# Branch projections as seven block products per pair of output tiles, with weight sums formed in DRAM, on one Trainium2 core

## The chip, the cores and the metric

The kernel runs on one core of a Trainium2 chip. The metric is the device time of one execution in microseconds (us). Before the change the median of 3 runs was 1196.73 us (1196.19 to 1196.98).

## What is computed

One layer of a decoder with 1024 positions and 1024 channels, in float32. The reference, cut to what the change touches:

```python
proj = h @ w_in[l]                      # h = rmsnorm(x)
q, k, v, su, sv, g_a, g_b = jnp.split(proj, splits, axis=-1)
y_att = sliding_window_attention(q, k, v, ...)         # 1024 x 512
y_sgu = chunked_spatial_gating(su, sv, ...)            # 1024 x 512
merged = (jax.nn.sigmoid(g_a) * (y_att @ w_oa[l])      # branch a
          + jax.nn.sigmoid(g_b) * (y_sgu @ w_ob[l]))   # branch b
x = x + merged @ w_out[l]
x = x + conv_gated_mlp(rmsnorm(x, ffn_norm[l]), ...)
```

The change rewrites the two products `y_att @ w_oa` and `y_sgu @ w_ob`, each 1024 x 512 by 512 x 1024.

## The kernel before, in words

Everything is kept transposed: channels on the 128 partitions, positions along the free dimension. A float32 product is made of three TensorE matmuls in the fp32r format: operands are split into a high part (`copy_hi`, ACT, L87) and a low part (operand minus high part, one subtraction on DVE or POOL), and `mm3` (L91 to L93) adds high·high, high·low and low·high in PSUM. One matmul is 128x128 by 128x512. PSUM is used as four rotating tiles of 128x1024 float32 (`PS`).

The program is written under a manual schedule: on each engine the instructions stand in the order in which the code issues them, and each engine runs its own list in that order. The stages, one after the other on TensorE:

1. Attention, the spatial gate and the input projections other than the gates (to about 247 us).
2. Gate projections, "gate pairs" 1 to 7 (`gate_pair`, called from `gates`). Each pair makes one tile of gate a (`zv`) and one of gate b (`zg`) by seven block products instead of eight (class `Blocks`, L1039 issues its matmuls; 12 matmuls in a product, 84 in a pair). Between products there are copies of PSUM halves to SBUF on ACT (`x1`, `x7`, `u2`; L1099, L1105, L1049), sums on DVE (L620, L1048, L1058), a scale on DVE (L1055) and a tanh on ACT (L1068, `gate_out`); the tanh goes to DRAM until its branch tile is merged. During pair 7, which has no successor to prepare, the right sides of the branch projections are split: `ys_split` for branch b (`bh` on ACT, `bl` on DVE, L1144) and `ya_split` for branch a (`ah` on ACT, `al` on POOL, L1144), four times 128x1024 each.
3. Branch projections: 16 jobs (`branch`), one tile of 128 output channels each, in the order b, b, a, a. A job is a plain contraction over 512 channels (`dense`: 4 steps of 128 channels, two halves of 512 positions, 3 matmuls: 24). DVE then multiplies by one plus the tanh (L1190, L1192), adds the two branches (L1193), and the merged tile is split again for the next stage (`m_split`: `mh` on ACT, `ml` on DVE, L1204).
4. Output projection: 8 jobs (`out_tile`) of 48 matmuls (L91 to L93, tile `px`), each followed by the residual sum, the norm's square and the splits for the MLP (`right_split`).
5. The MLP's up projection in block products (`first_pair`, then `fast_pair`, whose copies to `x1` and `x7` are L1501 and L1518), and the down projection.

`run_jobs` drives stages 3 and 4: job i's matmuls are issued, then job i + 4's weights are loaded (SP queue, tile `wj`) and job i + 2's are split (`wjh` on ACT, L87; `wjl` on POOL, L108), then the rest of job i.

Two things of the machine's use matter for reading the change. PSUM accumulation: in `Blocks` the product "A12·B21" is added onto the half `g0` that holds "A11·B11", after ACT has copied "A11·B11" out to `x1`; in the same way "A22·T4" is added onto `v0` after the copy to `x7`. TensorE therefore waits at its third product for ACT's copy `x1`, and at its fifth for `x7`. And in `fast_pair` ACT's copy to `x7` stands behind `nx.split_s3()`, the split of the next pair's weights.

Of the kernel before, what the change touches and what calls it, by code (L numbers as in the profile page):

```python
# [10 lines left out]
F = mybir.dt.float32  # L11
# [30 lines left out]
def body(ctx, tc, nc, a):  # L42
# [658 lines left out]
    def job_load(i):  # L701
        if i < len(jobs):
            src, nk, _ = jobs[i]
            job_w[i] = wload(src, "wj", nk) if nk else first_left()
            if not nk:
                next(job_w[i])

    def job_split(i):
        if i < len(jobs):
            nk = jobs[i][1]  # L710
            if nk:
                job_w[i] = wsplit(job_w[i], "wj", nk)
            else:
                for _ in job_w[i]:
                    pass
# [74 lines left out]
    def v_phase():  # L790
# [8 lines left out]
        for s in range(7):  # L799
# [5 lines left out]
            v_gelu(s)  # L805
            if s < 4:
                nc.scalar.activation(uT[:, s, :], uT[:, s, :], AF.Gelu_apprx_tanh)
# [15 lines left out]
    def v_end():  # L823
# [3 lines left out]
        v_half(7, 1)  # L827
        sgu_mm(1, 0)
# [70 lines left out]
    pools = {"dr": dr}  # L899

# [30 lines left out]
    class Left:  # L931
# [15 lines left out]
        def load_ahead(self):  # L947

            if "lq" not in pools:
                pools["lq"] = U("lq", F, (128, 2, 2048))  # L950
# [71 lines left out]
    class Blocks:  # L1022


        def __init__(self, w, y, z=None):
            self.w, self.y = w, y
            self.rest(z or (PS("pz"), PS("pz")))
# [7 lines left out]
        def prod(self, o, l, r, more=False):  # L1035
            (wh, wl), y = self.w[l], self.y[r]
            for k in range(4):
                for j, (p, q) in enumerate(((wh, 0), (wh, 1), (wl, 0))):
                    nc.tensor.matmul(o, p[:, k, :], y[:, q, k, :], start=not more and k == 0 and j == 0,  # L1039
                                     stop=k == 3 and j == 2, skip_group_check=True)  # L1040
# [39 lines left out]
    def gates_close():  # L1080
# [4 lines left out]
        pools["mg"] = pools["mg_cm"].__enter__()  # L1085

    def gate_pair(c, prev):
# [15 lines left out]
        gate_out(("b", c - 1), prev.zg)  # L1103
        q.prod(q.v0, "S3", "T3")
        nc.scalar.copy(x7, q.v0)  # L1105
        q.prod(q.g0, "A12", "B21", more=True)
# [4 lines left out]
        else:  # L1111
            ys_split()
            job_split(0)
            job_load(2)
        q.prod(q.g1, "S1", "T1")
        sub(nc.vector, x7, x7, q.g1)
        if nx:
            nx.sums_r()
        q.prod(q.v0, "A22", "T4", more=True)
        if nx:  # L1120
            nx.split_q()
        else:
            job_split(1)
            ya_split()
# [12 lines left out]
    yb = {}  # L1137

    def y_split(n, t, src, eng):
        if n not in yb:  # L1140
            yb[n] = Y(n + "h"), Y(n + "l")
        h, l = yb[n]
        copy_hi(h[:, t, :], src)
        eng.tensor_tensor(l[:, t, :], src, h[:, t, :].bitcast(F), op=ALU.subtract)  # L1144

    def ys_split():
        for t in range(4):
            y_split("b", t, uT[:, t, :], nc.vector)
# [5 lines left out]

    def ya_split():
        for t in range(4):
            y_split("a", t, yb["raw"][:, t, :], nc.gpsimd)

    def gates():
# [6 lines left out]
        for key in B_ORDER[:2]:  # L1166
            th_load(key)


    B_ORDER = [(br, c + e) for c in range(0, 8, 2) for br in "ba" for e in (0, 1)]  # L1170
    ms = {}

    def th_load(key):
        th[key] = pools["ls"].tile([128, 1024], F, tag="th", name=nm("th"), bufs=3)
        nc.sync.dma_start(th[key], d_th[key])

    def branch(n):
        br, c = B_ORDER[n]

        def main(w):  # L1180
            if n + 2 < 16:
                th_load(B_ORDER[n + 2])
            yh, yl = yb[br]
            p = PS("po")
            dense(p, *w, lambda k: yh[:, k, :], lambda k: yl[:, k, :], 4)
            yield
            t = th.pop((br, c))
            if br == "b":
                ms[c] = pools["mg"].tile([128, 1024], F, tag="m", name=nm("m"), bufs=3)
                nc.vector.scalar_tensor_tensor(ms[c], t, 1.0, p, op0=ALU.add, op1=ALU.mult)  # L1190
            else:
                nc.vector.scalar_tensor_tensor(p, t, 1.0, p, op0=ALU.add, op1=ALU.mult)  # L1192
                nc.vector.tensor_tensor(ms[c], ms[c], p, op=ALU.add)  # L1193
                m_split(c)
        jobs.append((a["wob" if br == "b" else "woa"][c], 4, main))
# [3 lines left out]
    def m_split(c):  # L1199
        if mhi[c // 4] is None:  # L1200
            mhi[c // 4], mlo[c // 4] = Y("mh"), (Y if c < 4 else U)("ml")
        h, l = mhi[c // 4][:, c % 4, :], mlo[c // 4][:, c % 4, :]
        copy_hi(h, ms[c])
        nc.vector.tensor_tensor(l, ms.pop(c), h.bitcast(F), op=ALU.subtract)  # L1204

    for n in range(16):
        branch(n)
# [4 lines left out]
    def open_out():  # L1212
# [4 lines left out]
        pools["ex"] = ctx.enter_context(tc.tile_pool(name="ex", bufs=1, reuse_waits="tile"))  # L1217
# [4 lines left out]
        comb["T3"] = pools["ex"].tile([128, 2, 4, 512], R, tag="T3", name="T3")  # L1222
# [6 lines left out]
        out_load(D_ORDER[0])  # L1229
# [15 lines left out]
    def out_tile(i):  # L1245
        d = D_ORDER[i]

        def main(w):
            if i == 0:
                open_out()  # L1250
            if i < 7:
                out_load(D_ORDER[i + 1])
            sq2, ac = pools["sq2"], acs.pop(d)
# [579 lines left out]
```

## Time and profile before

| what | value |
|---|---|
| median of the runs | 1196.73 us (1196.19 to 1196.98) |
| the profiled execution's own time | 1196.83 us |
| its span, first to last instruction | 1195.1 us |
| branch projections on TensorE (384 matmuls) | 380.6 to 467.7 us |
| gate pair 7 on TensorE (84 matmuls) | 361.5 to 380.6 us |
| output projection on TensorE (384 matmuls) | 467.7 to 554.9 us |
| busy share of the span | DVE 70%, ACT 45%, POOL 50% |

The page of the profile gives the busy time of each engine, the chain of work that ended last and the costliest groups of instructions; the trace behind it can be asked for single waits, groups of instructions and stretches of time. Times there count from the first instruction. The profiled execution's time is 1.7 us above its span.

### The profile page before, as it was taken

What the parts mean: (1) busy time and instruction counts of PE and PEld (TensorE: products, weight loads), DVE (VectorE), ACT (ScalarE), POOL (GpSimd) and SP (SyncE); (2) the same over time, 40 slices, a digit from 0 to 9 for tenths busy, and PEclk for the clock granted to TensorE, in tenths of its full rate; (3) what the DMA queues carried; (4) which work ended last, traced back from release to release, by engine and by line L of the source; (5) the groups of instructions that cost most, each with busy time, mean ns of one, the idle gap of its engine ahead of it and who ended that gap; (6) DMA issues with size and microseconds to landing.
All of it is one profiled execution on the core that took longest, in us unless ns stands there. A gap on an engine that the chain in (4) does not pass through costs nothing.

```text
span 1195.1 us, 15765 instructions
## 1 busy us (share of the span) xinstructions
PE 1181.0 (99%) x5890; PEld 1000.1 (84%) x5890; DVE 834.6 (70%) x984; ACT 540.9 (45%) x832; POOL 596.7 (50%) x408
## 2 busy tenths in 40 slices
PE   8999999999999999999999999999999999999998
PEld 8989989988888888888788888888888888888887
DVE  7798975752325453678787788878887798775674
ACT  8555567644435122235444435444444445434331
POOL 2367684587686222344777676767767551000000
PEclk9999999999999999999999999999999999999999
DMA  7110143024343634353555555545545358975472
GB/s 273 34 54 19 54 142 124 13 94 141 108 174 106 219 134 159 124 175 110 129 159 138 135 166 134 167 119 146 155 137 146 92 203 282 367 247 194 151 227 72
DMA packets 72797, 173.97 MB, mean 146 GB/s; under 512 B 8208, under 2 KB 8464, under 8 KB 72720
## 3 DMA queue, kind: packets, MB, share of 16 engines
q1 hardware_dynamic: 66384, 161.42, 39.0%
q0 software_dynamic: 6336, 11.54, 6.5%
q8 instruction: 46, 0.75, 0.3%
q14 instruction: 31, 0.25, 0.1%
HBM read 133.87 MB, written 39.06 MB: 145 GB/s over the span
## 4 chain that ended last, share of the span: by engine, by line
PE 85%; DVE 5%; POOL 2%; ACT 1%; issue 1%; DMA 0%; POOLq 0%; ACTq 0%; DVEq 0%
PE pz L1039 43%; PE pd L1659 10%; PE pdy L1659 8%; PE px L92 2%; PE po L93 2%; PE po L92 2%; PE px L93 2%; PE px L91 2%; PE po L91 2%; PE pvs L92 1%; PE pvs L91 1%; PE pvs L93 1%; PE pu L93 1%; PE pu L91 1%; PE pu L92 1%
## 5 line engine op out<-in xcount | busy, mean ns | idle before, releaser
L1039 PE MATMUL pz<-T,qh 128*128 128x512 f32 x472 | 145.7, 390 | 1.7 <-ACT x L1518 1.7
L1039 PE MATMUL pz<-B,ph 128*128 128x512 f32 x352 | 109.7, 393 | 0.2
L1039 PEld LDWEIGHTS pz<-T,qh 128*128 128x128 f32 x472 | 88.4, 188 | 20.7 <-ACT x L1518 2.1
L999 POOL TENSOR_TENSOR pl<-lp,ph 128x1024 fp32r<-128x1024 f32 x30 | 73.1, 2437 | 54.4 <-ACT ph L87 54.4
L1039 PE MATMUL pz<-T,ql 128*128 128x512 f32 x236 | 91.8, 389 | 0.0
L108 POOL TENSOR_TENSOR wjl<-wj,wjh 128x512 fp32r<-128x512 f32 (+1 forms) x24 | 39.9, 1663 | 99.1 <-ACT wjh L87 94.9
L999 POOL TENSOR_TENSOR ql<-lq,qh 128x1024 fp32r<-128x1024 f32 x30 | 76.6, 2552 | 9.1 <-ACT qh L87 9.1
L1039 PEld LDWEIGHTS pz<-B,ph 128*128 128x128 f32 x352 | 65.0, 188 | 16.6 <-ACT x L1501 3.8
L1055 DVE TENSOR_TENSOR pz<-pz,rstd_b 128x1024 f32<-128x1024 f32 x60 | 73.9, 1232 | 4.6 <-ACT rstd_b L141 2.5
L1039 PE MATMUL pz<-T,s3h 128*128 128x512 f32 x232 | 71.4, 389 | 0.0
L1039 PE MATMUL pz<-B,pl 128*128 128x512 f32 x176 | 68.6, 390 | 0.0
L1659 PE MATMUL pd<-bh,ah 128*128 128x512 f32 x176 | 68.5, 389 | 0.0
L1659 PE MATMUL pd<-bh,al 128*128 128x512 f32 x176 | 68.5, 389 | 0.0
L1659 PE MATMUL pd<-bl,ah 128*128 128x512 f32 x176 | 68.5, 389 | 0.0
L1039 PE MATMUL pz<-T,AX 128*128 128x512 f32 x264 | 63.4, 389 | 0.0
L1039 PE MATMUL pz<-B,AX 128*128 128x512 f32 x264 | 63.4, 389 | 0.0
L1039 PEld LDWEIGHTS pz<-T,AX 128*128 128x128 f32 x264 | 49.5, 188 | 10.3
L1039 PEld LDWEIGHTS pz<-B,AX 128*128 128x128 f32 x264 | 49.6, 188 | 10.3
L999 POOL TENSOR_TENSOR s3l<-lq,s3h 128x512 fp32r<-128x512 f32 x20 | 25.9, 1296 | 63.0 <-ACT s3h L87 63.0
L1359 DVE SCALAR_TENSOR_TENSOR tg<-pz,cp,tg 128x1023 f32<-128x1023 f32 (+1 forms) x44 | 56.2, 1277 | 0.8
L1359 DVE SCALAR_TENSOR_TENSOR tv<-pz,cp,tv 128x1023 f32<-128x1023 f32 (+1 forms) x44 | 56.2, 1277 | 0.8
L87 ACT ACTIVATE AX<-lr 128x1024 fp32r<-128x1024 f32 x22 | 23.4, 1063 | 71.0 <-POOL lr L620 71.0
(344 smaller groups left out, 3547.5 us busy)
## 6 DMA issues: line engine op xcount, KB each, us to landing
lp<-wup SPq DMA_DIRECT2D x22, 512.0 KB, 3.8
lq<-wup SPq DMA_DIRECT2D x22, 512.0 KB, 4.0
ra<-wdown SPq DMA_DIRECT2D x44, 256.0 KB, 4.5
b<-T SPq DMA_DIRECT2D x44, 256.0 KB, 3.8
lq<-wup POOLq DMA_DIRECT2D x42, 256.0 KB, 5.2
B<-tv SPq DMA_DIRECT2D x33, 256.0 KB, 2.0
T<-tt SPq DMA_DIRECT2D x33, 256.0 KB, 2.2
b<-B SPq DMA_DIRECT2D x33, 256.0 KB, 3.2
```

What stands on the lines that cost most here:

```text
L87: return nc.scalar.activation(dst, src, AF.Copy, scale=scale)
L91: nc.tensor.matmul(out, wh, mh, start=first, stop=False, **kw)
L92: nc.tensor.matmul(out, wh, ml, start=False, stop=False, **kw)
L93: nc.tensor.matmul(out, wl, mh, start=False, stop=last, **kw)
L108: nc.gpsimd.tensor_tensor(l[:, :nk, :], r[:, :nk, :], h[:, :nk, :].bitcast(F), op=ALU.subtract)
L999: nc.gpsimd.tensor_tensor(l, r, h.bitcast(F), op=ALU.subtract)
L1039: nc.tensor.matmul(o, p[:, k, :], y[:, q, k, :], start=not more and k == 0 and j == 0, stop=k == 3 and j == 2, skip_group_check=True)
L1055: nc.vector.tensor_tensor(z, z, rstd_b, op=ALU.mult)
L1359: nc.vector.scalar_tensor_tensor(t[:, j:], p[:, 0:1024 - j], cw[:, ci, 2 - j:3 - j], t[:, j:], op0=ALU.mult, op1=ALU.add)
L1659: nc.tensor.matmul(o[d], p[:, k - k0, m], q[:, k - k0, :], start=new and k == 0 and j == 0, stop=k == HK - 1 and j == 2, skip_group_check= ...
```

## The change

1. **Branch projections.** The 16 jobs become 8 units, in the order b, a, b, a and so on. A unit makes two neighbouring output tiles of one branch by seven block products with 2 steps of 128 channels: 7 x 6 = 42 matmuls, where two jobs of before had 48. It is two jobs: the first with the products A11·B11, S3·T3, A12·B21 and S1·T1, the second with A22·T4, S2·T2 and S4·B22. Between them stand the copies `x1`, `x7` and `u2` on ACT (L1280, L1282, L1299 of the changed kernel) and the sums on DVE; PSUM tiles are called `pz` here too.
2. **Weight sums.** S1 to S4 come from DRAM. `wb_copy` copies the 512 KB blocks of the weights to a DRAM tile (8 times, on ACT's queue, in stage 1); `wb_add` adds the other blocks onto it by accumulating transfers (6, on POOL's queue, one in each of the gate pairs 1 to 6).
3. **Right sides.** The seven right sides of each branch (B11, B21, B22, T1 to T4) are sums of quarters (`y_sum`, DVE, 128x1024 each) and are split by `y_split` (`copy_hi` on ACT, the low part on DVE or POOL; L1213). Branch b's sums stand in gate pairs 3 to 6; branch a's sums and ten of the fourteen splits in gate pair 7; the last four splits (a: T3, T1, T2, T4) behind pair 7 in `gates`, ahead of the first unit.
4. **Merge and output tiles.** The low parts of the merged tiles go to POOL in halves, one job later (`m_add`, `m_lo`), those of the last unit stay on DVE. Output tiles 0 and 1 are first contracted over steps 0 to 5 of 8, then over 6 and 7 (`rest`), and the split of job 18 moves.
5. **MLP's start.** The buffers `T3` and `lq` trade places. `lefts[2].load_ahead()` and `adds()` stand earlier in `first_pair`, and in the first call of `fast_pair` (`rms` set) the copy to `x7` stands ahead of `nx.split_s3()`.

Gate pair 7 and the first unit on **ACT**. `bh`, `ah` and `y...` are high parts of right sides, `uT`, `ya` and `yt` their sources, `wjh` the high parts of weights, `x`, `u` the copies of PSUM halves, `th` the tanh of a gate tile. Before, from the copy `x7` of pair 7 to the first weights of the branch stage:

```order
L1105 COPY x_498_3913<-pz_3911 128x512
L87 ACTIVATE bh_3965<-uT_683 128x1024 x4
L87 ACTIVATE wjh_3975<-wj_3929 128x512
L87 ACTIVATE wjh_4006<-wj_3931 128x512
L87 ACTIVATE ah_4010<-ya_3741 128x1024 x4
L1049 COPY u_499_3914<-pz_3911 128x512
L1068 ACTIVATE th_4039<-pz_3911 128x1024
L1068 ACTIVATE th_4057<-pz_3910 128x1024
L87 ACTIVATE wjh_4099<-wj_3979 128x512
```

And now, from the last weights split in pair 7 to the first unit's two copies (L1280 is its `x1`, L1282 its `x7`):

```order
L87 ACTIVATE wjh_4046<-wj_3959 128x256
L1068 COPY u_502_3939<-pz_3936 128x512
L87 ACTIVATE y_515_4072<-uT_683 128x1024
L87 ACTIVATE y_515_4072<-yt_3694 128x1024
L1087 ACTIVATE th_4081<-pz_3936 128x1024
L87 ACTIVATE y_519_4097<-uT_683 128x1024
L87 ACTIVATE y_519_4097<-ya_3764 128x1024
L1087 ACTIVATE th_4105<-pz_3935 128x1024
L87 ACTIVATE y_524_4123<-ya_3764 128x1024 x2
L87 ACTIVATE y_525_4128<-ya_3764 128x1024 x2
L1280 COPY x_528_4135<-pz_4133 128x512
L1282 COPY x_529_4136<-pz_4134 128x512
```

Between pair 7's last tanh (`th_4105`) and the first unit's copies there now stand four splits of 128x1024; the tanh tiles themselves now have splits between them.

The same place on **DVE**. `bl` and the second name of `y` rows are low parts; `ya<-ya` rows are the sums of branch a; `pz` rows with L1048/L1067, L620 and L1058/L1077 are pair 7's sums in PSUM, those with `rstd_b` its scales. Before, all of pair 7's tail up to the first merge of a branch tile (L1190):

```order
L1144 TENSOR_TENSOR bl_3966<-uT_683,bh_3965 128x1024 x4
L620 TENSOR_TENSOR x_498_3913<-x_498_3913,pz_3910 128x512
L1048 TENSOR_TENSOR pz_3911<-x_497_3912,pz_3911 128x512
L620 TENSOR_TENSOR pz_3911<-pz_3911,u_499_3914 128x512
L620 TENSOR_TENSOR pz_3911<-x_498_3913,pz_3911 128x512
L1055 TENSOR_TENSOR pz_3911<-pz_3911,rstd_b 128x1024
L1058 TENSOR_TENSOR pz_3910<-u_499_3914,pz_3910 128x512
L1055 TENSOR_TENSOR pz_3910<-pz_3910,rstd_b 128x1024
L1190 SCALAR_TENSOR_TENSOR m_4103<-th_4066,po_4072 128x1024
```

And now, in two pieces that follow each other, from the first split to the scale of `zv`:

```order
L1213 TENSOR_TENSOR y_507_3983<-uT_683,y_507_3983 128x1024
L1213 TENSOR_TENSOR y_507_3983<-yt_3560,y_507_3983 128x1024
L620 TENSOR_TENSOR x_501_3938<-x_501_3938,pz_3935 128x512
L1213 TENSOR_TENSOR y_512_4029<-uT_683,y_512_4029 128x1024
L1213 TENSOR_TENSOR y_512_4029<-yt_3426,y_512_4029 128x1024
L620 TENSOR_TENSOR ya_3764<-ya_3764 128x2x512 x2
L624 SCALAR_TENSOR_TENSOR ya_3764<-ya_3764 128x2x512
L1067 TENSOR_TENSOR pz_3936<-x_500_3937,pz_3936 128x512
L620 TENSOR_TENSOR pz_3936<-pz_3936,u_502_3939 128x512
L620 TENSOR_TENSOR pz_3936<-x_501_3938,pz_3936 128x512
L1074 TENSOR_TENSOR pz_3936<-pz_3936,rstd_b 128x1024
```

and from there to the first instruction of unit 0:

```order
L1213 TENSOR_TENSOR y_515_4072<-uT_683,y_515_4072 128x1024
L1213 TENSOR_TENSOR y_515_4072<-yt_3694,y_515_4072 128x1024
L1213 TENSOR_TENSOR y_519_4097<-uT_683,y_519_4097 128x1024
L1213 TENSOR_TENSOR y_519_4097<-ya_3764,y_519_4097 128x1024
L620 TENSOR_TENSOR ya_3764<-ya_3764 128x2x512
L1077 TENSOR_TENSOR pz_3935<-u_502_3939,pz_3935 128x512
L1074 TENSOR_TENSOR pz_3935<-pz_3935,rstd_b 128x1024
L1213 TENSOR_TENSOR y_524_4123<-ya_3764,y_524_4123 128x1024 x2
L620 TENSOR_TENSOR x_529_4136<-x_529_4136,pz_4133 128x512
```

The last scale (L1055 before, L1074 now) is followed by the tanh of `zg`. From the first split to that scale DVE had 11 instructions and now has 19, eight of them splits and four sums of `ya`. On POOL, in the same place, stand three 512-wide and one 256-wide subtractions for `wjl` and two 128x1024 splits of branch a, and behind them the splits of `y_525`.

The first call of `fast_pair` on **ACT**, with `s3h`, `ph`, `qh` the next pair's weights and `x` (L1518 before, L1673 now) the copy to `x7`. Before:

```order
L1354 ACTIVATE tv_5514<-pz_5318,cp 128x1024
L1354 ACTIVATE tg_5528<-pz_5319,cp 128x1024
L87 ACTIVATE s3h_5546<-lq_5457 128x512
L1518 COPY x_685_5512<-pz_5321 128x512
L87 ACTIVATE ph_5553<-lp_5455 128x1024
```

And now:

```order
L1510 ACTIVATE tv_5681<-pz_5485,cp 128x1024
L1510 ACTIVATE tg_5695<-pz_5486,cp 128x1024
L1673 COPY x_714_5679<-pz_5488 128x512
L87 ACTIVATE s3h_5714<-lq 128x512
L87 ACTIVATE ph_5720<-lp_5627 128x1024
```

The copy has changed places with the split `s3h`.

The diff, cut to its core:

```diff
@@ run_jobs
         for i in range(len(jobs) - 1):
             m = jobs[i][2](job_w.pop(i))
             next(m)
+            if i == 17:
+                job_split(18)
+                next(m)
             job_load(i + 4)
-            job_split(i + 2)
+            if i != 16:
+                job_split(i + 2)
             for _ in m:
                 pass
+            if lo_late:
+                lo_late.pop(0)()
@@ v_phase, v_end: wb_copy(s) behind v_gelu(s) for s = 0..6, wb_copy(7)
+    def wb_copy(j):
+        br, i = divmod(j, 4)
+        o, x = ((1, 0), (1, 1), (0, 0), (0, 1))[i]
...
+        nc.scalar.dma_start(d_wb[br, o][128 * x:128 * x + 128], a["wb"][br, o + x])
+    def wb_add(j):
...
+        nc.gpsimd.dma_start(out, src, accum_op=ALU.add, max_dma_last_dim=4096)
@@ gate_pair
         gate_out(("b", c - 1), prev.zg)
+        if nx:
+            wb_add(c - 1)
+        if 2 < c < 7:
+            y_sum("b", ("T1", "T3", "T2", "T4")[c - 3])
         q.prod(q.v0, "S3", "T3")
         nc.scalar.copy(x7, q.v0)
+        if not nx:
+            y_split("b", "B11")
+            y_split("b", "T3")
         q.prod(q.g0, "A12", "B21", more=True)
...
-            ys_split()
             job_split(0)
             job_load(2)
+            y_split("a", "B11", nc.gpsimd)
+            y_split("a", "B22", nc.gpsimd)
         q.prod(q.g1, "S1", "T1")
         sub(nc.vector, x7, x7, q.g1)
...
+            y_split("b", "B21")
+            y_split("b", "T1")
         q.prod(q.v0, "A22", "T4", more=True)
...
             job_split(1)
-            ya_split()
+            y_sum("a", "T1")
+            y_sum("a", "T3")
+            y_sum("a", "T2")
...
         q.sums(x1, x7, q.v0)
         if not nx:
+            y_split("b", "T4")
+            y_split("b", "T2")
             job_load(3)
         gate_out(("a", c), q.zv)
         q.prod(q.g1, "S4", "B22", more=True)
+        if not nx:
+            y_split("b", "B22")
+            y_split("a", "B21")
+            y_sum("a", "T4")
@@ gates
         gate_out(("b", 7), q.zg)
         gates_close()
+        th_load(0)
+        y_split("a", "T3")
+        y_split("a", "T1")
+        y_split("a", "T2", nc.gpsimd)
+        y_split("a", "T4", nc.gpsimd)
@@ branch
+        def first(w):
...
+            q.prod(q.g0, "A11", "B11")
+            nc.scalar.copy(x1, q.g0)
+            q.prod(q.v0, "S3", "T3")
+            nc.scalar.copy(x7, q.v0)
+            q.prod(q.g0, "A12", "B21", more=True)
+            q.prod(q.g1, "S1", "T1")
             yield
+            sub(nc.vector, x7, x7, q.g1)
+            if un["late"]:
+                un["late"]()
+        def second(w):
...
+            q.prod(q.v0, "A22", "T4", more=True)
+            q.prod(q.v1, "S2", "T2")
+            nc.vector.tensor_tensor(q.v1, x1, q.v1, op=ALU.add)
+            nc.scalar.copy(q.u2, q.v1)
+            sub(nc.vector, q.v0, q.v0, q.u2)
+            sub(nc.vector, q.v1, x7, q.v1)
+            q.prod(q.g1, "S4", "B22", more=True)
+            yield
+            nc.vector.tensor_tensor(q.g1, q.u2, q.g1, op=ALU.add)
...
+    B_PARTS = (("A11", "S3", "A12", "S1"), ("A22", "S2", "S4"))
+    for u in range(8):
+        for part in (0, 1):
+            branch(u, part)
@@ out_tile
-            dense(p, *w, lambda k: mhi[k // 4][:, k % 4, :], lambda k: mlo[k // 4][:, k % 4, :], 8)
+            if i < 2:
+                dense(p, *w, mh, ml, 8, range(6))
+                rest.append((p, *w, mh, ml, 8, (6, 7)))
+                if i == 0:
+                    rest.append(lambda: post(p, ac))
+                else:
+                    dense(*rest[0])
+                    yield
+                    dense(*rest[2])
+            else:
+                dense(p, *w, mh, ml, 8)
@@ fast_pair
         q.prod(q.v0, "S3", "T3")
+        if rms:
+            nc.scalar.copy(x7, q.v0)
         if nx:
             nx.split_s3()
...
-        nc.scalar.copy(x7, q.v0)
+        if not rms:
+            nc.scalar.copy(x7, q.v0)
```

More of the change, by code (lines that the diff above doesn't have):

```diff
@@ L702, in job_load @@
         if i < len(jobs):
[L703 to L706, printed above, removed]
+            job_w[i] = jobs[i][0]()
     def job_split(i):
         if i < len(jobs):
[L710 to L715, printed above, removed]
+            job_w[i] = jobs[i][1](job_w[i])
+    lo_late = []
     def run_jobs():
@@ L805, in v_phase @@
             v_gelu(s)
+            wb_copy(s)
             if s < 4:
@@ L827, in v_end @@
         v_half(7, 1)
+        wb_copy(7)
         sgu_mm(1, 0)
@@ L1197, in body @@
-    mhi, mlo = [None, None], [None, None]
[L1199 to L1207, printed above, removed]
+        th_load(0)
+        y_split("a", "T3")
+        y_split("a", "T1")
+        y_split("a", "T2", nc.gpsimd)
@@ L1326, in body @@
     late = {}
+    rest = []
     for i in range(8):
@@ L1425, in first_pair @@
         w, nx = lefts[0], lefts[1]
+        pools["mr_cm"].__exit__(None, None, None)
+        pools["ex"] = ctx.enter_context(tc.tile_pool(name="ex", bufs=1, side="right", reuse_waits="tile"))
         z = PS("pz"), PS("pz")
@@ L1757, in mlp, with left_begin, left_end @@
                 q.tanh()
-    jobs.append((None, 0, None))
+    def left_begin():
+        m = first_left()
+        next(m)
+        return m
+    def left_end(m):
+        for _ in m:
+            pass
+    jobs.append((left_begin, left_end, None))
     with tc.manual_schedule():
@@ L1807, in layout @@
         "wgb": tiles(w_in[:, 2816:3840], 8),
-        "woa": tiles(w_oa[qcols], 4),
-        "wob": tiles(w_ob, 4),
+        "wb": c(np.stack([pairs(w_ob), pairs(w_oa[qcols])])),
         "wout": tiles(w_out, 8),
```

190 lines of the change are left out of this document (140 added, 50 removed).

## The prediction

> **What bounds the kernel now.** I read first the busy shares and the clock, then TensorE's waits, then the branch stage and gate pair 7 on the other engines. From the page:
>
> ```profile
> PE 1181.0 (99%) x5890; PEld 1000.1 (84%) x5890; DVE 834.6 (70%) x984; ACT 540.9 (45%) x832; POOL 596.7 (50%) x408
> PE 85%; DVE 5%; POOL 2%; ACT 1%; issue 1%; DMA 0%; POOLq 0%; ACTq 0%; DVEq 0%
> ```
>
> TensorE (PE) is busy for 99% of the span and is 85% of the chain that ended last. So matmuls removed from an undisturbed stage count in full, and any wait put into it counts in full too. The two largest of PE's waits (total, times, longest):
>
> ```profile
> PE pkv L91 <- ACT x L87: 2.2, 2, 1.9
> PE pz L1039 <- ACT x L1518: 1.7, 1, 1.7
> ```
>
> The first lies at the kernel's start, the second in the first `fast_pair`. None stands in the gate pairs or the branch stage. The branch stage, as the first and the last group of tile `po` (min/median/max ns, first and last start):
>
> ```profile
> L91 PE MATMUL po<-bh,wjh x64: 389/389/389, 380.6 to 456.1; 128*128 128x512 f32 x64
> L93 PE MATMUL po<-ah,wjl x64: 389/389/389, 392.0 to 467.4; 128*128 128x512 f32 x64
> ```
>
> 384 matmuls start from 380.6 to 467.4: 86.8 / 383 = 0.2267 us apart, without a gap. The duration of 389 ns is pipelined; the spacing is the price.
>
> **The change, part by part.**
>
> *Matmuls.* 8 units of 42 are 336 instead of 384: 48 x 0.2267 = **-10.88 us**.
>
> *The wait at 590 us.*
>
> ```profile
> 588.09 0.39 PE L1039 MATMUL pz<-T,ql 128*128 128x512 f32 x1
> 589.03 0.63 ACT L87 ACTIVATE s3h<-lq 128x512 fp32r<-128x512 f32 x1 [3.27 <-DMA lq<-wup]
> 589.57 0.57 ACT L1518 COPY x<-pz 128x512 f32<-128x512 f32 x1
> 590.19 0.73 PE L1039 MATMUL pz<-T,qh 128*128 128x512 f32 x2 [1.71 <-ACT x L1518]
> ```
>
> ACT was idle until the load of `lq` landed, split it, and only then made the copy that PE needed. PE's step is 2.10 us instead of 0.23. With the copy ahead of the split it goes: **-1.87 us**. The split starts 0.6 us later at most, under a whole pair of matmuls.
>
> *Entry into unit 0.* PE finishes pair 7 where `po` begins, at 380.62, and runs two products of 6 matmuls, 2 x 1.36 us. The third, A12·B21, is added onto the half that ACT must first copy out (`x1`), so PE is there at 380.62 + 2.72 = 383.34. By the order of ACT's list, that copy stands behind everything pair 7's end now issues: two tanh, eight splits, and the four splits of `gates`. The last tanh needs DVE's last scale, and DVE's list ahead of it grew to 19 instructions. So the question is when DVE ends. Durations, in pair 7 and the branch stage by group (count, busy and mean ns), and for `bl` by its tile:
>
> ```profile
> L108 POOL TENSOR_TENSOR wjl<-wj,wjh 128x512 fp32r<-128x512 f32 x16 | 20.8, 1297 | 60.1 <-ACT wjh L87 55.9 <-DMA wj<-wob 4.2
> L1144 POOL TENSOR_TENSOR al<-ya,ah 128x1024 fp32r<-128x1024 f32 x4 | 9.5, 2406 | 0.0
> L1055 DVE TENSOR_TENSOR pz<-pz,rstd_b 128x1024 f32<-128x1024 f32 x4 | 4.9, 1232 | 0.1
> L1068 ACT ACTIVATE th<-pz 128x1024 f32<-128x1024 f32 x4 | 4.1, 1026 | 6.4 <-DVE pz L1055 6.4
> L87 ACT ACTIVATE ah<-ya 128x1024 fp32r<-128x1024 f32 x4 | 3.9, 1044 | 0.0
> L620 DVE TENSOR_TENSOR pz<-pz,u 128x512 f32<-128x512 f32 x1 | 0.7, 700 | 1.6 <-ACT u L1049 1.6
> L1099 ACT COPY x<-pz 128x512 f32<-128x512 f32 x1 | 0.6, 587 | 0.3 <-PE pz L1039 0.3
> L1144 DVE TENSOR_TENSOR bl<-uT,bh x4: 1210/1222/2315, 370.0 to 374.5; 128x1024 fp32r<-128x1024 f32 x4
> ```
>
> An undisturbed split lasts 1.22 us and the next starts about 0.07 us before its end, 1.15 us a piece; a sum of `ya` has the same size, so I give it the same. DVE's 19: 12 x 1.15 + 5 x 0.70 + 2 x 1.2 = 19.7 us. It starts where the high part of the first right side is there:
>
> ```profile
> 367.22 0.59 ACT L1105 COPY x<-pz 128x512 f32<-128x512 f32 x1 [0.20 <-PE pz L1039]
> 370.01 5.73 DVE L1144 TENSOR_TENSOR bl<-uT,bh 128x1024 fp32r<-128x1024 f32 x4 [4.99 <-PE pz L1039]
> 372.21 1.31 POOL L108 TENSOR_TENSOR wjl<-wj,wjh 128x512 fp32r<-128x512 f32 x1 [3.62 <-ACT wjh L87]
> ```
>
> The copy `x7` ends at 367.81, one split on ACT later it is 368.85. Laid out row by row, DVE also waits for others: two splits end at 371.15, `x7` minus `g1` waits for PE's fourth product (the copy at 367.22 read the second, two more of 12 x 0.2267 end at about 372.4), the next split for its high part on ACT (behind four splits and two `wjh`, 374.3), and smaller ones: 3.3 us in all. If nobody else stood in its way, DVE would end at 368.85 + 19.7 + 3.3 = 391.9. But POOL does: of the four `bl`, the one beside the `wjl` at 372.21 to 373.52 lasted 2315 ns, 1.1 us longer than its brothers and until one split's length behind POOL's end. The same again in the output stage, and for contrast a case of a DVE instruction that reads PSUM:
>
> ```profile
> 479.71 2.39 POOL L108 TENSOR_TENSOR wjl<-wj,wjh 128x1024 fp32r<-128x1024 f32 x1 [8.48 <-ACT wjh L87]
> 480.00 3.17 DVE L1268 SCALAR_TENSOR_TENSOR h<-ac,cp,rstd_b 128x1024 f32<-128x1024 f32 x1
> 397.68 1.30 POOL L108 TENSOR_TENSOR wjl<-wj,wjh 128x512 fp32r<-128x512 f32 x1 [4.15 <-DMA wj<-wob]
> 398.46 1.22 DVE L1193 TENSOR_TENSOR m<-m,po 128x1024 f32<-128x1024 f32 x1
> L1193 DVE TENSOR_TENSOR m<-m,po x8: 1220/1220/1222, 398.5 to 469.1; 128x1024 f32<-128x1024 f32 x8
> ```
>
> `h` has only SBUF operands and lost about two microseconds beside POOL (it too ends one split's length, 1.1 us, behind POOL's end at 482.10); `m<-m,po` has one operand in PSUM and, beside POOL's `wjl`, lasted what all eight of its kind last. In pair 7 POOL now has three 512-wide `wjl`, one of 256 and two 128x1024 splits: 3 x 1.30 + 0.65 + 2 x 2.40 = 9.35 us, all at times when DVE has a split or a sum of `ya` at the head of its list. If they take turns, the works add: 368.85 + 19.7 + 9.35 = 397.9 (the waits of the undisturbed walk fall into POOL's turns). Behind it ACT needs the tanh (1.03), four splits (4 x 0.98, by the 3.9 us of four) and the copy (0.59): 5.5 us, and PE goes on at 403.4. **Stall: 403.4 - 383.34 = +20.1 us.** Without turns it is 391.9 + 5.5 - 383.34 = 14.1; with DVE never waiting for anything, 388.55 + 5.5 - 383.34 = 10.7, the floor. I take 20.1, since three rows show the turns.
>
> The Trainium skill, "SBUF — State Buffer", section "🔬 SBUF: two separate sides", says that VectorE and GpSimd share a port pair under an exclusive lock for the whole instruction, where a VectorE instruction with two SBUF inputs meets a GpSimd one that reads SBUF. It speaks against this change, which gives splits to both engines in one stretch: by the rule the stall is the 20.1, without it 14.1. The rows of `h` and `m<-m,po` agree with it, also where it makes the exception.
>
> *PE's clock after the stall.* Granted clock (PEclk) around the early gap:
>
> ```profile
> core 0: us, PE busy (x) PEld busy (x) DVE busy (x) ACT busy (x) POOL busy (x), PEclk, DMA share, GB/s
> 5.00:10.00 5.00, 3.36 (x15) 2.75 (x16) 2.96 (x6) 3.77 (x9) 0.00 (x0) 0.83 1.01 362
> 10.00:20.00 10.00, 10.00 (x83) 10.00 (x82) 10.00 (x19) 10.00 (x20) 0.00 (x0) 0.92 0.78 297
> ```
>
> These 15 us lost 0.17 x 5 + 0.08 x 10 = 1.65 us of clock, in and behind a stretch in which PE was idle for 1.64 of 5 us. A stall of 14 to 20 us has no row; the bounds are nothing and twice this. I take **+1.6 us**. The Trainium skill, "TensorE: Matmul & The Clock Gate", Part 1, has the clock halved after an idle window of about 3.4 us and restored after as much work; an estimate from it is half of 3.4, 1.7 us, near to the row and without effect on the sum.
>
> *Units 1 to 7.* Unit length on PE 42 x 0.2267 = 9.52 us. DVE has five sums of 512 and two merges (5 x 0.70 + 2 x 1.22 = 5.9 us), for branch a two more (8.4); all have an operand in PSUM, so POOL doesn't hold them, by the row of `m<-m,po`. `x1` is copied 1.36 us after its product ends, behind at most two weight splits. I take 0.
>
> *Output tiles 0 to 2.*
>
> ```profile
> 478.57 1.06 ACT L87 ACTIVATE wjh<-wj 128x1024 fp32r<-128x1024 f32 x1 [7.12 <-PE px L92]
> ```
>
> Tile 2's weights can only be split when tile 0's rest has been read: 1.06 us on ACT and 2.40 on POOL (the 2.39 above) against tile 1's rest of 12 x 0.2267 = 2.72 us and two matmuls of tile 2 that need no low part (0.45): 3.56 - 3.17, **+0.5 us** rounded up; from nothing to 0.9. The interleaving itself costs no matmul and covers the splits of the last merged tiles, which otherwise end too late.
>
> *Weight sums.* The trace shows no transfer from DRAM to DRAM. The nearest rows are an issue on SP, an issue of an accumulating transfer on POOL, and POOL's idle time in the gate pairs and the MLP:
>
> ```profile
> 399.00 0.33 SPq L97 DMA_DIRECT2D wj<-woa  x1
> 591.56 1.16 POOL L958 DMA_DIRECT2D lq<-wup  x1
> L999 POOL TENSOR_TENSOR pl<-lp,ph 128x1024 fp32r<-128x1024 f32 x30 | 73.1, 2437 | 54.4 <-ACT ph L87 54.4
> ```
>
> Eight issues on ACT are 8 x 0.33 = 2.6 us at most, in a stage in which ACT is not what PE waits for longest; one issue of 1.16 us on POOL per gate pair fits into the 54.4 / 30 = 1.8 us for which POOL stands idle ahead of each `pl`. The last addition, in pair 6, lands ahead of the branch stage unless it takes over 19 us, pair 7's length. I take 0, with 0 and 2.6 as ends.
>
> **The sum**, against the profiled execution's 1196.83 (0.1 above the median, so no correction): 1196.83 - 10.88 - 1.87 + 20.1 + 1.6 + 0.5 = **1206.3 us**, slower.
>
> **The rivals.**
>
> *A: no turns.* DVE and POOL work side by side in pair 7. For it: three of four `bl` took 1.22 us. Against it: the 2315 ns of the one that met POOL. Stall 14.1: 1206.3 - 6.0 = 1200.3, and 1198.7 if the clock holds.
>
> *B: the entry is hidden, and the kernel gets faster.* One mechanism: PE doesn't stand at A12·B21, because the copy `x1` comes in time. It decides at 383.34: DVE's last scale would have to end by 377.8, where before, with 11 instructions, it ended at 384.97:
>
> ```profile
> 383.74 1.23 DVE L1055 TENSOR_TENSOR pz<-pz,rstd_b 128x1024 f32<-128x1024 f32 x1
> ```
>
> Then 1196.83 - 12.75 + 0.5 = 1184.6. Against it stands the floor of 10.7 us; for it only that I followed the lists by hand. Below a stall of 10.65 us (12.75 - 0.5 - 1.6) the kernel is no longer slower.
>
> *C: unit 1 waits too.* POOL's two splits of `y_525` (a: T2, T4) stand ahead of the weights of unit 1. They start near 402.9 and take 4.8 us, 2.3 more if DVE's two splits of `y_524` come in between, then two `wjl`, 2.6: 412.6, where unit 1 is due at 403.4 + 5 x 1.36 = 410.2. +2.4: 1208.7. For it: POOL's list; against: DVE's splits start first, and the first `wjl` alone lets PE start.
>
> *D: it doesn't do what it says.* Sums in DRAM that land late would show as waits of `wjh` for a DMA. A unit would wait for each; with pair 7 to spare I give it no chance of its own.
>
> **How the numbers follow.** Forecast with turns 0.55; C 0.15; A 0.16; B 0.14. The measurement tells 0.2% (2.4 us) from no change. Slower by more: forecast, C and somewhat over half of A (1200.3 with the clock's loss, not 1198.7): 0.79. Within 0.2%: the rest of A, 0.07. Faster: B, 0.14. The range leaves out B and the very end of C: from A's lower value less 1.2 us (half of the open 2.6 us of DVE's waits), 1197.5, to C with the upper ends of clock and tile 2 (1208.7 + 1.6 + 0.4), 1210.7.
>
> **What would show it.** In the profile after: a wait of PE at the third product of unit 0 for ACT's `x` (L1280) of 14 to 21 us, one only; `y` splits on DVE of over 2 us beside POOL's; granted clock under 1 in the stage behind it; 336 matmuls otherwise 0.2267 apart; no wait for L1673. If the wait is under 10 us, my walk through DVE's list is wrong. If PE waits in every unit, the units' lists are.

## The result and the profile after

The change made the kernel slower: 1213.49 us (median of 4 runs, 1212.38 to 1214.4) against 1196.76 us; the ratio is 1.014 (95% interval 1.0123 to 1.0158). The profiled execution took 1212.38 us, its span is 1210.7. The forecast was slower too, 1206.3 us, but its range ended at 1210.7, 2.8 us below the measured time: the sign and the main mechanism were right, and one wait was missing.

The page of the changed kernel, the same two lines as before:

```profile
PE 1172.4 (97%) x5842; PEld 992.1 (82%) x5842; DVE 869.9 (72%) x1032; ACT 566.4 (47%) x878; POOL 637.0 (53%) x442
PE 62%; POOL 1%; ACT 1%; DVE 1%; issue 1%; DMA 0%; POOLq 0%; ACTq 0%
```

TensorE has 48 matmuls fewer and is busy for 8.6 us less, yet the span is 15.6 us longer. Its waits (total, times, longest) say where that is:

```profile
PE pz L1058 <- ACT x L1280: 19.2, 1, 19.2
PE px L91 <- DVE m L1331: 5.8, 1, 5.8
PE pkv L91 <- ACT x L87: 1.9, 1, 1.9
```

Two new waits, one time each. The first is the forecast one: unit 0's third product waits for the copy `x1`. In the order of time:

```profile
381.96 0.39 PE L1058 MATMUL pz<-y,wjl 128*128 128x512 f32 x1
...
394.88 1.23 DVE L1074 TENSOR_TENSOR pz<-pz,rstd_b 128x1024 f32<-128x1024 f32 x1
396.20 1.02 ACT L1087 ACTIVATE th<-pz 128x1024 f32<-128x1024 f32 x1 [4.79 <-issue]
397.12 3.88 ACT L87 ACTIVATE y<-ya 128x1024 fp32r<-128x1024 f32 x4
400.90 0.57 ACT L1280 COPY x<-pz 128x512 f32<-128x512 f32 x1
401.53 1.22 PE L1058 MATMUL pz<-y,wjh 128*128 128x512 f32 x2 [19.18 <-ACT x L1280]
402.55 0.63 PE L1058 MATMUL pz<-y,wjl 128*128 128x512 f32 x1
```

DVE's last scale, the last tanh, the four splits, the copy: each starts when the one above it ends. The matmuls behind the wait are 0.43 us apart instead of 0.23, until 405.5. The second wait was not forecast:

```profile
476.69 0.39 PE L1058 MATMUL pz<-y,wjl 128*128 128x512 f32 x1
...
481.49 1.21 DVE L1331 TENSOR_TENSOR m<-m,pz 128x1024 f32<-128x1024 f32 x1
482.74 1.06 ACT L87 ACTIVATE mh<-m 128x1024 fp32r<-128x1024 f32 x1 [4.66 <-DVE m L1331]
482.85 0.77 PE L91 MATMUL px<-mh,wjh 128*128 128x512 f32 x1 [5.77 <-DVE m L1331]
483.41 0.63 PE L92 MATMUL px<-ml,wjh 128*128 128x512 f32 x1
483.84 0.63 PE L93 MATMUL px<-mh,wjl 128*128 128x512 f32 x1
```

The first matmul of output tile 0 starts when DVE has read the first PSUM tile (`pz`) of unit 7. It starts before ACT's `mh` of that merge ends (482.74 + 1.06), so it isn't the merged data that it waits for.

From profile to profile, where a step is the time from one matmul's start to the next one's: matmuls -10.88; the wait in unit 0 19.57 - 0.23 = +19.35 and slow matmuls behind it +1.9; the wait of output tile 0 6.16 - 0.23 = +5.9 and slow matmuls behind it +2.1; output tile 2 +0.4; the MLP's start -1.7. That is +17.1, and 15.6 was measured. 1.16 us of the difference arose ahead of the branch stage, where pair 7's last matmul starts at 380.40 us before and at 379.24 now. The slow clock at 8 to 12 us, which the profile of before has (0.83 and 0.92 granted) and that of the changed kernel has not, leaves 0.7 of it at 180 us. From 186 to 217 us matmuls of 256 columns stand 0.118 us apart before and 0.113 now, another 1.2, of which a wait at 217 us takes most back. Neither belongs to the change: the profile of experiment 4, the kernel before with one edit, has no slow clock at 8 to 12 us and 0.113, that of experiment 1 has the slow clock (0.83 and 0.91) and 0.118. The last 0.3 us lies in the MLP. The clock at the start and in unit 0, in the profile of the changed kernel:

```profile
core 0: us, PE busy (x) PEld busy (x) DVE busy (x) ACT busy (x) POOL busy (x), PEclk, DMA share, GB/s
5.00:10.00 5.00, 3.68 (x19) 3.66 (x20) 3.42 (x7) 4.22 (x10) 0.00 (x0) 1.00 1.01 403
10.00:20.00 10.00, 9.79 (x86) 9.59 (x85) 10.00 (x19) 10.00 (x21) 0.00 (x0) 1.00 0.82 296
380.60:410.00 29.40, 10.22 (x37) 8.00 (x36) 18.26 (x18) 12.47 (x16) 8.94 (x5) 0.65 0.37 125
```

### The profile page after: what moved, and what is told of

It is laid out like the page before. It is cut to its first block, busy times and chain, and to the rows that moved or that the text cites. A ratio compares the mean times of both kernels' runs of the same rounds, so it can differ in the third digit from the quotient of the medians.

```text
span 1210.7 us, 15917 instructions
## 1 busy us (share of the span) xinstructions
PE 1172.4 (97%) x5842; PEld 992.1 (82%) x5842; DVE 869.9 (72%) x1032; ACT 566.4 (47%) x878; POOL 637.0 (53%) x442
## 4 chain that ended last, share of the span: by engine, by line
PE 62%; POOL 1%; ACT 1%; DVE 1%; issue 1%; DMA 0%; POOLq 0%; ACTq 0%
PE pz L1058 38%; PE pd L1820 10%; PE pdy L1820 7%; PE px L91 2%; PE px L93 2%; PE px L92 2%; DMA lq<-wup 0%; POOL pl L1017 0%; POOL lr L620 0%; ACT T L87 0%; ACT y L87 0%; DVE res L1840 0%; DVE pz L1313 0%; POOL ql L1017 0%; DVE pz L620 0%
## 5 line engine op out<-in xcount | busy, mean ns | idle before, releaser
L1058 PE MATMUL pz<-T,qh 128*128 128x512 f32 x472 | 145.6, 390 | 0.0
L1058 PE MATMUL pz<-B,ph 128*128 128x512 f32 x352 | 109.6, 392 | 0.3 <-ACT x L1660 0.3
L1058 PEld LDWEIGHTS pz<-T,qh 128*128 128x128 f32 x472 | 88.4, 188 | 18.7 <-ACT u L883 0.3
L1058 PE MATMUL pz<-T,ql 128*128 128x512 f32 x236 | 91.8, 389 | 0.0
L1058 PE MATMUL pz<-y,wjh 128*128 128x512 f32 x224 | 70.4, 396 | 19.2 <-ACT x L1280 19.2
L1058 PEld LDWEIGHTS pz<-B,ph 128*128 128x128 f32 x352 | 65.1, 188 | 16.2 <-ACT x L1660 3.2
L1074 DVE TENSOR_TENSOR pz<-pz,rstd_b 128x1024 f32<-128x1024 f32 x60 | 73.9, 1232 | 4.6 <-ACT rstd_b L141 2.5
L1058 PE MATMUL pz<-T,s3h 128*128 128x512 f32 x232 | 71.4, 389 | 0.0
L1058 PE MATMUL pz<-B,pl 128*128 128x512 f32 x176 | 68.6, 390 | 0.0
L1058 PEld LDWEIGHTS pz<-y,wjh 128*128 128x128 f32 x224 | 42.9, 192 | 28.5 <-ACT x L1280 19.6
L1058 PE MATMUL pz<-T,AX 128*128 128x512 f32 x264 | 63.4, 389 | 0.0
L1058 PE MATMUL pz<-B,AX 128*128 128x512 f32 x264 | 63.4, 389 | 0.0
L620 DVE TENSOR_TENSOR x<-x,pz 128x512 f32<-128x512 f32 x36 | 24.5, 681 | 51.7 <-PE pz L1058 43.9
L1058 PEld LDWEIGHTS pz<-T,AX 128*128 128x128 f32 x264 | 49.6, 188 | 10.3
L1058 PEld LDWEIGHTS pz<-B,AX 128*128 128x128 f32 x264 | 49.6, 188 | 10.3
```

What stands on the lines that cost most here:

```text
L620: eng.tensor_tensor(out, x, y, op=op)
L1058: nc.tensor.matmul(o, p[:, k, :], m, start=not more and k == 0 and j == 0, stop=k == nk - 1 and j == 2, skip_group_check=True)
L1074: nc.vector.tensor_tensor(z, z, rstd_b, op=ALU.mult)
```

## The experiments

**1. Another PSUM buffer for output tile 0.** The pools of PSUM tiles rotate, and `open_out` swaps one place, so that output tile 0 gets the pool of the last tiles written. When a job made one tile, that pool's older buffer belonged to the last job but one. When a unit makes two tiles, it is unit 7's first.

```diff
-        psum["P"].insert(0, psum["P"].pop())
+        psum["P"] = psum["P"][0::2] * 2
...
             p = PS("px")
+            if i == 1:
+                psum["P"].append(psum["P"].pop(2))
```

> The changed kernel, but output tile 0 takes the PSUM buffer of unit 6 (long read) and output tile 1 that of unit 7's first tile, instead of the other way round; all other tiles keep their buffers. Theory 'buffer': PE's 5.8 us wait ahead of output tile 0 is for DVE's merge of unit 7's first tile, because tile 0 was given exactly that PSUM buffer. Then the wait goes, with the ten slow matmuls behind it: 6.2 + 2.0 us, so about 1205.3 us where the changed kernel has 1213.5; the wait of unit 0 stays at 19 us. Rival 'merge too late': the merged tiles themselves come too late for the contraction; then PE waits for mh or ml instead, by 3 us or more, and the time stays above 1209.

Measured: 1206.32 us (1205.55 to 1206.38), ratio to before 1.0079 (1.0064 to 1.0094). No wait for L1331 is left; output tile 0 follows the last unit in step:

```profile
478.28 0.39 PE L1058 MATMUL pz<-y,wjl 128*128 128x512 f32 x1
478.50 0.39 PE L91 MATMUL px<-mh,wjh 128*128 128x512 f32 x1
478.73 0.39 PE L92 MATMUL px<-ml,wjh 128*128 128x512 f32 x1
```

7.2 us went with one buffer: the theory "buffer" holds, and the rival, merged tiles too late, is out. The expected 8.2 us did not come back in full: behind unit 0 the slow matmuls lost 2.5 us here, 1.9 in the changed kernel. With this wait removed the kernel stands at the forecast's 1206.3; that the two agree so closely is luck, since single terms were off by more.

**2. The four splits of branch a behind unit 0's copies.** In ACT's list only: the `y_split` lines of `gates` are issued in `first`, for unit 0, behind its `x1` and `x7`.

> The changed kernel, but the four splits of branch a that stood ahead of unit 0 (T3, T1, T2, T4) are issued behind unit 0's copies x1 and x7. Theory 'ACT's list': the copy x1 follows the last tanh directly, 4 x 0.98 us earlier, so PE's wait in unit 0 falls from 19.2 to 15.3 us and the time by 3.9 to about 1209.6; unit 1 begins 6.8 us behind the copy and finds its right sides. Rival 'the work itself is late': the splits are needed for unit 1 at once, PE waits there for what it gained, and the time changes by less than 1 us.

Measured: 1210.5 us (1209.52 to 1211.05). The wait in unit 0 (L1276 here) and the next largest:

```profile
PE pz L1058 <- ACT x L1276: 15.4, 1, 15.4
PE px L91 <- DVE m L1332: 5.8, 1, 5.8
```

19.2 became 15.4: the four splits are 3.8 us of the wait, by their place in the list. Of the time 3.0 of the expected 3.9 us came back; part of the rest is a new wait of unit 1 for its weights, which POOL makes behind branch a's last two splits, rival C of the prediction at a smaller price:

```profile
PE pz L1058 <- POOL wjl L1262: 0.6, 1, 0.6
```

**3. POOL's two splits in gate pair 7 on DVE.**

```diff
-            y_split("a", "B11", nc.gpsimd)
-            y_split("a", "B22", nc.gpsimd)
+            y_split("a", "B11")
+            y_split("a", "B22")
```

> The changed kernel, but the low parts of branch a's B11 and B22 are made on DVE instead of POOL in gate pair 7. Theory 'turns': DVE and POOL exclude each other here, so 2 x 2.4 us of POOL's work leave the chain and 2 x 1.15 enter it: PE's wait in unit 0 falls from 19.2 to about 16.8 us, no split on DVE in pair 7 lasts over 2.6 us, and the time falls by about 2.5 to 1211. Rival 'no turns': DVE, with two more splits, ends 2.3 us later, and the wait grows to 21.5 us, the time to about 1215.8.

Measured: 1210.93 us (1210.2 to 1213.3), the wait 17.2 us. DVE got two more splits and was done earlier. The changed kernel, DVE and POOL in pair 7:

```profile
372.37 5.75 POOL L1213 TENSOR_TENSOR y<-ya,y 128x1024 fp32r<-128x1024 f32 x2
372.64 3.22 DVE L1213 TENSOR_TENSOR y<-uT,y 128x1024 fp32r<-128x1024 f32 x1 [0.45 <-ACT y L87]
375.79 3.41 DVE L1213 TENSOR_TENSOR y<-yt,y 128x1024 fp32r<-128x1024 f32 x1
378.07 3.96 POOL L1266 TENSOR_TENSOR wjl<-wj,wjh 128x512 fp32r<-128x512 f32 x2
379.12 3.99 DVE L620 TENSOR_TENSOR ya<-ya 128x1024 f32<-128x1024 f32 x2
```

and the experiment:

```profile
371.54 3.73 DVE L1213 TENSOR_TENSOR y<-ya,y 128x1024 fp32r<-128x1024 f32 x2 [0.74 <-ACT y L87]
375.55 2.98 POOL L1266 TENSOR_TENSOR wjl<-wj,wjh 128x512 fp32r<-128x512 f32 x2 [1.36 <-ACT wjh L87]
375.79 2.14 DVE L1213 TENSOR_TENSOR y<-uT,y 128x1024 fp32r<-128x1024 f32 x1
377.85 1.76 DVE L1213 TENSOR_TENSOR y<-yt,y 128x1024 fp32r<-128x1024 f32 x1
```

Beside POOL's splits a DVE split lasted 3.2 and 3.4 us; without them the longest took 2.3 us, beside POOL's `wjl` (the second of the two in the first row). The two engines take turns: the rival, 21.5 us, is out. The Trainium skill, "SBUF — State Buffer", section "🔬 SBUF: two separate sides", states this as an exclusive lock for the whole instruction; these rows agree, by 2 us that left the wait when 2 x 2.4 us left POOL and 2 x 1.2 came to DVE.

**4. One edit alone: the copy `x7` of the first fast pair, in the kernel before.** The edit is the last hunk of the diff.

> The kernel before, with one edit of the change alone: in the first call of the MLP's fast pairs ACT's copy x7 stands ahead of the split s3h. Theory: the wait of 1.7 us at 590 us goes, and nothing takes its place: 1194.9 us, 1.9 less than before. Rival: the split, now 0.6 us later, is awaited in its turn by POOL and PE, and less than 0.5 us is gained.

Measured: 1197.36 us (1196.71 to 1197.79, 10 runs) against 1196.7 (13 runs), ratio 1.0005 (0.9995 to 1.0014): nothing gained, where 1.9 us was expected. The wait at 590 us is gone and a longer one stands in the next pair:

```profile
PE pz L1039 <- ACT x L1501: 3.0, 1, 3.0
```

PE is there 1.9 us earlier, but ACT's copy for the next pair (starts at 603.27 us) stands behind the first tap of a convolution (602.17), which needs DVE's scale (600.90), that a sum, that ACT's copy `u`, which stands behind `AX` (597.87), and that POOL's sums `lr` (end at 597.84). Their chain starts at the load of `lq` that ACT had been waiting for.

**5. The same edit taken back in the changed kernel** (with the buffer of experiment 1).

> The changed kernel with the PSUM buffer of output tile 0 as in the first experiment, and in the first call of the MLP's fast pairs ACT's copy x7 again behind the split s3h. Theory 'copy': with the loads of the changed kernel the copy matters, PE waits for it again by 1 to 2 us, and the time rises to about 1208. Rival 'POOL's chain': the copy alone brought nothing to the kernel before, because the next pair waited for POOL's sums instead; here too it changes less than 0.5 us.

Measured: 1206.59 us (1205.21 to 1207.24) against 1206.32 in experiment 1. PE's step in the first fast pair is 0.89 us instead of 0.23, that of the next pair 0.51 instead of 1.09: the rival holds. So in the changed kernel 1.2 of the 1.87 us at 590 us go without the copy. ACT's wait for the load of `lq` there is 2.06 us instead of 3.27, which fits the loads that the change issues earlier; no run tests them alone.

**6. Output tiles 0 and 1 contracted at once** (with the buffer of experiment 1): `rest` and the moved split of job 18 undone.

> The changed kernel with the PSUM buffer of output tile 0 as in the first experiment, but output tiles 0 and 1 contracted over all 8 steps at once, as before the change. Theory: step 7 of tile 0 comes 9.5 us after the last unit, DVE's last low part 11.6 us after it, so PE waits about 2 us in tile 0 (with some slow clock), and tile 2's wait of 0.4 us goes: 1.5 to 3 us more than the first experiment, 1208 to 1209. Rival: the interleaving covers nothing, and the time is that of the first experiment, 1206.3, or 0.4 less.

Measured: 1207.12 us (1206.45 to 1207.65), 0.8 us above experiment 1; the intervals of the two ratios overlap, so the times alone show no difference. The profile shows what was expected, smaller: two waits in tile 0 for the merged tiles (steps of 1.11 and 1.26 us, 1.9 us lost), and tile 2's step of 0.66 us gone. The interleaving covers about 1.5 us there.

**7. The lists around unit 0 in another order** (with the buffer of experiment 1). Unit 0's first two products and its copies (`begin`) are issued ahead of pair 7's scales and tanh, everything of branch a behind them; `lo` issues the low part of the split above it:

```diff
+            lo = y_split("b", "B22", None)
+            nc.vector.tensor_tensor(q.v1, x1, q.v1, op=ALU.add)
+            begin(job_w[0], lambda: nc.scalar.copy(q.u2, q.v1))
+            lo()
...
+            gate_out(("a", c), q.zv)
```

> The changed kernel with the PSUM buffer of output tile 0 as in the run before, and with the same copies, sums and splits around unit 0 in another order: unit 0's first two products and the copies x1 and x7 stand ahead of pair 7's scales and tanh, these ahead of everything of branch a, and branch a's splits are all on DVE. Units still go b, a, b, a. Theory 'place in the list': unit 0 waits under 1 us; unit 1 (branch a) then comes too early for its right sides and waits some 2 to 8 us in all; about 1190 us. Rival 'amount of work': DVE's work is what it was, so unit 1 waits for nearly all that unit 0 no longer waits for, and the time stays above 1200.

**8. The same, and the units in the order b, b, a, a, b, a, b, a.**

> As the run with the reordered lists, and the units in the order b, b, a, a, b, a, b, a, so that branch a is first needed 9.5 us later (the low parts of merged tiles on POOL are issued faster where more than three wait). Theory: no wait of PE of over 1 us from gate pair 7 to output tile 2, and no slow clock there: the change's own gain shows, 10.9 us of matmuls and about 1 us in the MLP's start: 1185 us, 1183 to 1188. Rival: with 8 units in a row some chain of DVE, ACT or POOL is longer than PE's 9.5 us a unit, and waits of some 1 us come back in each unit: above 1190.

Measured: 1202.62 us (1201.69 to 1204.94) and 1203.03 us (1201.96 to 1203.19), 12.6 and 18 us above the two expectations. The first is in the range of its rival (above 1200), but the wait is not the one in unit 1 that the rival named. Both have the same large wait:

```profile
PE pz L1058 <- DVE x L620: 16.9, 1, 16.9
```

```profile
PE pz L1060 <- DVE x L620: 16.9, 1, 16.9
```

It is no longer unit 0's third product but its last, S4·B22, which overwrites the PSUM half that DVE's `x7` minus `g1` must read first, and that row stood behind the whole block of branch a in DVE's list. One row of a unit behind the block is enough.

**9. Branch a's work spread** over the ends of units 0 and 1, the order of units as in 8.

> As the run with the units in the order b, b, a, a, b, a, b, a, but branch a's sums and splits no longer stand in one block ahead of unit 0's own sums on DVE (there unit 0's x7 minus g1, which its last product needs, waited for the block): they are spread behind the sums of units 0 and 1, four of the splits' low parts on DVE and three on POOL. Theory 'place in the list': what PE waited for in the two runs before was only this, so no wait of over 1 us stays in unit 0; unit 2, the first of branch a, may wait 1 to 3 us for its last right sides; 1186 us (1184 to 1189), the first version below the kernel before. Rival 'amount of work': DVE has some 25 us of work for units 0 and 1 and branch a's right sides in 19 us, so the wait moves to units 1 and 2 by 5 us or more, with slow clock: 1192 or above.

Measured: 1197.85 us (1196.12 to 1199.46, 11 runs), ratio 1.0009 (1.0000 to 1.0018). That is what the rival expected (1192 or above, over 5 us of waits in units 1 and 2, slow clock). Unit 0 has no wait of over 1 us; in unit 1 two steps of 1.3 and 1.2 us appear, and in unit 2 PE waits again for the copy `x1`, and again ACT's list holds two splits ahead of it that wait for DVE's sums:

```profile
PE pz L1060 <- ACT x L1279: 8.5, 2, 8.3
```

**10. The same, finer:** those two splits behind unit 2's copies, DVE's merges of unit 1 behind them.

> As the run with branch a's work spread out, in a finer order: branch a's splits of T4 and T2 are issued on ACT behind unit 2's copies x1 and x7 (in the run before these copies stood behind them, and PE waited 8.3 us for x1), DVE's last sum and merges of unit 1 stand behind them, and B11 and B22 are split on DVE behind unit 0's sums. Theory 'place in the list': the wait of 8.3 us and the slow clock behind it go, some 3 to 4 us of short waits for branch a's right sides stay in unit 2: 1190 us (1188 to 1192), below the kernel before. Rival 'amount of work': DVE and POOL need the time that PE waits, whatever the order; PE waits 7 us or more in units 0 to 2 in all, and the time stays within 0.2% of before.

Measured: 1195.47 us (1194.36 to 1196.11, 11 runs), ratio 0.9989 (0.9979 to 0.9998): just below the kernel before, 18 us below the changed one, but 5 us above the expectation. The largest waits:

```profile
PE pz L1060 <- DVE y L1216: 3.0, 2, 2.7
PE pz L1060 <- DVE x L620: 2.6, 1, 2.6
```

All steps above 0.5 us in units 0 to 2 lose 7.8 us, and two stretches of slow matmuls another 3 us. By both of its signs, 7 us or more of waits and a time within 0.2% of before, the rival "amount of work" came out, though the 8.3 us ahead of `x1` went as the other theory expected.

**11. The same, with branch a's four sums left out.**

> The finer order of the run before, with branch a's four sums of right sides left out of the computation (its products take the unsummed quarters): 4 x 1.15 us less work on DVE, the order of everything else as it was. In the run before PE still waited some 8 us in units 1 and 2, mostly for DVE's splits of branch a and for DVE's x7 minus g1, with slow clock behind. Theory 'amount of work': these waits are DVE's work, so they shrink by about the 4.6 us left out and the slow clock of 3 us shrinks with them: 1195.5 falls to 1188 to 1190. Rival 'place in the list': the waits hang on single rows that stand too late, the sums among the least of them; less than 2 us is gained, 1193.5 or above.

Measured: 1192.81 us (1189.67 to 1194.17), 2.7 us less, between the 4.6 us and more of the one theory and the 2 us of the other. The same steps now lose 5.3 us, and one of the two slow stretches is gone. So DVE's amount of work is part of what is left in experiment 10, but one wait of 3.1 us in unit 2 stayed (it was 2.8), which the sums don't explain. A row that is left out takes its work and its place in the list with it, so this run does not fully part the two theories. What the rest consists of stays open.

## Why the prediction was right and where it failed

- **Matmuls, -10.88 us.** Right: 42 a unit, 0.2267 us apart; between 405.5 and 476.7 us no step is over 0.3 us. The units themselves wait for nothing.
- **Entry into unit 0, +20.1 us.** Right in mechanism: 19.35 us, a wait for DVE's last scale, the tanh, four splits and the copy. The size was right partly by luck. The prediction booked all 9.35 us of POOL's work as turns and put DVE's own waits at nothing beside them. In the trace the turns lengthen DVE's rows by 5.8 us (splits and sums that start at 372.64 to 381.46), since POOL's first two `wjl` cost DVE almost nothing (they run while it makes its first two splits and then waits for PE), and 2.7 us of DVE's waits (1.50 ahead of 371.50, 0.45 and 0.71 later) stand beside the turns: 8.5 for 9.35. Without turns an estimate from these rows is 19.35 - 5.8 = 13.5, near rival A's 14.1. Experiment 2 shows the place in ACT's list, experiment 3 the turns of DVE and POOL. Rival A (no turns) is out, rival B (hidden entry) didn't happen, and rival C (unit 1 waits for POOL) shows in experiment 2 alone, with 0.6 us.
- **PE's clock, +1.6 us** behind that wait. Measured 1.9 (1.4 to 2.5 behind the same wait in experiments 1, 5 and 6); but a second wait had a slow stretch of its own, 2.1. The row at 5 to 20 us that the size was taken from is not steady: the same stage has a granted clock of 1.00 in experiment 4, so the size was right partly by luck.
- **Output tiles 0 to 2, +0.5 us: this is the step that failed.** It asked when tile 2's weights could be split and when the last merged tiles were ready, and both answers hold (0.4 us at tile 2; experiment 6), though its first sum has a slip: 1.06 + 2.40 is 3.46, not 3.56. It did not ask which PSUM buffer tile 0 writes into. That is set by a line which the diff does not show as changed, `psum["P"].insert(0, psum["P"].pop())`; what changed is the number of tiles that a job takes from the rotation. 5.9 us of wait and 2.1 of clock were missing, and so the sign "one only" did not hold; experiment 1 returns 7.2.
- **The wait at 590 us, -1.87 us.** It went as predicted, but "under a whole pair of matmuls" was no proof that nothing is late next: by experiments 4 and 5 the copy alone is worth nothing, since POOL's chain in the next pair sets the end. In the changed kernel and in experiments 1, 5 and 6 some 0.7 to 1.7 us were gained by the whole change there.
- **Weight sums, 0.** No wait for them shows. The eight issues on ACT took 0.50 us or more each, over 4 us in all and more than the 2.6 of the upper end, but PE waited for none: the 0.5 us for ACT at 217 us shows in experiment 4 too, which has no weight sums.

With the buffer term the sum would have been 1206.3 + 8.0 = 1214.3, against 1213.49. The range's lower end takes "the open 2.6 us of DVE's waits", where the walk itself has 3.3; nothing hangs on it here.

## What to carry to other kernels

When a job begins to take two buffers of a rotation instead of one, write down for the stage behind it which buffer each tile gets and who reads it last; unchanged code can pick a worse one. Where engines run lists in order, a copy that TensorE waits for has the price of everything issued ahead of it, including what those rows wait for on other engines, and a block of preparation put "behind the last use" of one stage stands ahead of the first need of the next. Removing a wait is worth what the next chain leaves of it, so look one pair further before booking it.

## What the runs showed of the hardware

A wait's price has a second part, and its size varies. In the changed kernel TensorE's matmuls ran 0.427 us apart from 401.5 to 405.5 us, behind 19.35 us without work, and from 482.9 to 487.5 us, behind 5.9 us; in experiment 10 they did so from 401.4 to 404.8 us, behind 2.75 us. That lost 1.9, 2.1 and 1.6 us. Over all runs the loss behind waits of over 5 us is 1.4 (experiment 5) to 2.8 us (experiment 7), and it does not grow with the wait. Behind about 3 us it can be nothing: in experiment 4 PE stood for 3.1 us (the step of 3.36 us at 600.54), no slow stretch followed, and the granted clock was 1.00 from 600 to 605 us. The Trainium skill, "TensorE: Matmul & The Clock Gate", Part 1, has half the clock after an idle window of about 3.4 us and full clock after as much work. The slow stretches of 3.0 to 5.7 us behind these longer waits are about as long as the second says or longer; experiment 4 agrees with the first, and the drop behind 2.75 us of idling in experiment 10 came earlier than it says. The slow clock at 8 to 12 us, present in one profile and absent in the other, also shows that one profile's sum is uncertain by about 1 us.
